# Splitting the first normalisation over two engines, and the last product into three token ranges

## The chip, the core and the metric

The kernel runs on one core of a Trainium2 chip. The core has a matrix engine (TensorE, PE in the rows; its weight loads are PEld), a vector engine (VectorE, DVE), a scalar engine (ScalarE, ACT), a general engine (GpSimd, POOL), and a sync engine (SyncE, SP) that issues transfers; ScalarE and GpSimd issue transfers too. Each engine runs its own instructions strictly in order and waits on semaphores for the others. The metric is the device time of one execution in microseconds, as the median of several runs.

## What is computed

One step of a two-layer decoder in float32, for a prompt of 1024 tokens and a sample group of 8 × 4 tokens with the same weights. The first layer mixes tokens by retention, the second by sliding-window attention; each sub-layer is normalised before and after, and each layer ends in a feed-forward block:

```python
def rms_norm(x, g):
    xf = x.astype(jnp.float32)
    y = xf * lax.rsqrt(jnp.mean(xf * xf, axis=-1, keepdims=True) + EPS)
    return y.astype(x.dtype) * g.astype(x.dtype)
...
def retention_layer(h, pos, state0, g_pre, w_in, w_out, g_post):
    x = rms_norm(h, g_pre)
    proj = x @ w_in
    ...
    return h + rms_norm(o @ w_out, g_post), S

def ffn(h, g_pre, w1, w2, g_post):
    u = jax.nn.relu(rms_norm(h, g_pre) @ w1)
    return h + rms_norm((u * u) @ w2, g_post)
```

D_MODEL is 1024, the hidden width 4096. The two places that matter here are the very first `rms_norm(h, g_pre)` of the retention layer, for the first half of the prompt, and the very last line, `h + rms_norm((u * u) @ w2, g_post)` of the second layer, for the second half of the prompt and the sample group.

## The kernel before

The prompt is cut into two halves of 512 tokens; the second half carries the 32 sample tokens along, so it has 544 columns. Activations lie with features on the partitions and tokens along the columns, in 8 tiles of 128 features. A float32 product is made of three products of a reduced format (`passes`): high part with high part, high with low, low with high. ScalarE casts a weight tile to its high part (`whi`, line 499), VectorE subtracts for the low part (`wlo`, line 500). `proj_fm` (line 527) issues the three passes for each of 4 or 8 weight tiles of an output tile. The order on each engine follows from program order, a scheduler that respects the waits, and generators (`side`, `tick`) that let side work advance between products. PSUM has four banks for accumulators (`mm`) and four for transposes and the like (`aux`).

**The start.** Eight products of zeros (`RATES["warm"]`, line 208) run first. `x_first` then normalises four chunks of 128 tokens: a square with a row sum on ScalarE (line 566), small steps on VectorE, the scaling of the chunk (line 572), then for each half `q` of the features four transposes on TensorE (line 554), the multiplication by the gain on VectorE (line 578, 128 × 512), the cast to the high part on ScalarE (line 580) and the low part on VectorE (line 581). The results of two chunks feed products of 256 columns. Next to it the first weights arrive and are split (lines 499, 500).

**The tokens.** Before the last product, `tokens_of_h` reads the residual of the second half back and transposes it (line 1052) to rows of tokens, chunk by chunk, eight transposes for each.

**The last product.** `finish` adds the last block of hidden features to the accumulated result `y`. It goes over two ranges of tokens, 0 to 272 and 272 to 544. For each range and each of 8 output tiles `m`: 12 products (line 527), the addition to `y` on VectorE (line 538), on ScalarE the result times the gain (line 1096) and its square (line 1098), on VectorE the sum of squares (line 1100). From the fourth tile on, `turn` transposes finished tiles (line 1065) into six banks, two for each of three chunks of tokens; those of tiles 5 to 7 come after the last product of a range. `close` then sums the squares over the partitions by products of one column (line 1070), computes the factor with one activation (line 1075) and three small steps (lines 1076 to 1078), and for each chunk makes two additions of 512 columns on VectorE (line 1081) and one store (line 1087), from SyncE or ScalarE in turn. The close of the first range is written after the second tile of the second range. The chunks are 96, 96 and 80 tokens in the first range, 120, 120 and 32 in the second.

Of the kernel before, what the change touches and what calls it, by code (L numbers as in the profile page):

```python
# [13 lines left out]
AF = mybir.ActivationFunctionType  # L14
# [5 lines left out]
P = 128  # L20
# [96 lines left out]
def body(ctx, tc,  # L117
# [11 lines left out]
    def f32(ap):  # L129
        return ap.bitcast(F32)  # L130
# [76 lines left out]
    for _ in range(RATES["warm"]):  # L207
        T.matmul(wps[:, :256], lhsT=zero[:, :P], rhs=zero, start=True, stop=True)
# [348 lines left out]
    def x_first(xs, rp):  # L557

        loads = [x_load(0, c) for c in range(2)]
        for c in range(4):  # L560
# [13 lines left out]
            for q in range(2):  # L574
                pv = x_transpose(xn, q, P)
                d = slice(c * P, (c + 1) * P)
                tmp = rp.tile([P, 512], F32, tag="ob", bufs=3, name="xg").rearrange("p (k t) -> p k t", k=4)
                V.tensor_tensor(out=tmp, in0=pv, in1=g_first[:, 4 * q:4 * q + 4].unsqueeze(2).to_broadcast([P, 4, P]),
                                op=ALU.mult)
                S.copy(out=xs[q][0][:, :, d], in_=tmp)  # L580
                V.tensor_tensor(out=xs[q][1][:, :, d], in0=tmp, in1=f32(xs[q][0][:, :, d]), op=ALU.subtract)
            yield
# [452 lines left out]
    def token_chunks(r):  # L1035
        c0, c1 = RANGES[1][r]
        cut = [c0, 96, 192, c1] if r == 0 else [c0, 392, HC, c1]
        return list(zip(cut, cut[1:]))

    def tokens_of_h():  # L1040
# [3 lines left out]
        for r, (c0, c1) in enumerate(RANGES[1]):  # L1044
            h = range_tile(c1 - c0)
            G.dma_start(out=h, in_=hD[1][:, :, c0:c1])
            for i, (t0, t1) in enumerate(token_chunks(r)):
                yield out
                for q in range(2):
# [3 lines left out]
                    (S.copy if q else V.tensor_copy)(out=out[3 * r + i][:t1 - t0, q], in_=ps[:t1 - t0])  # L1053
        yield out

    def finish(f, hT):
# [10 lines left out]
        def close(st):  # L1067
# [4 lines left out]
            for i, (t0, t1) in enumerate(st["chunks"]):  # L1072
# [10 lines left out]
                if t0 < HC:  # L1083
                    dst = y_prompt[0, HC + t0:HC + t1]
                else:
                    dst = y_sample.rearrange("b t d -> (b t) d")
                (nc.sync, nc.scalar)[i % 2].dma_start(out=dst.rearrange("t (a c) -> t a c", a=2), in_=ht[:n])

        prev = None
        for r, (c0, c1) in enumerate(RANGES[1]):  # L1090
            w = c1 - c0
            st = dict(c0=c0, chunks=token_chunks(r), yg=range_tile(w), i0=3 * r, acc=nt()[:, :w])
            for m in range(KT):
# [9 lines left out]
                if m == 3:  # L1103
                    banks = [auxps() for _ in range(4)] + [mmps() for _ in range(2)]
                    st["outs"] = [banks[2 * i:2 * i + 2] for i in range(3)]
                    turn(st, 0)
# [473 lines left out]
```

## Time and profile before

| What | us |
|---|---|
| Median of 3 runs | 2871.67 |
| Lowest and highest | 2870.13, 2872.47 |
| Profiled execution | 2868.01 |
| Its span | 2866.2 |
| TensorE busy | 2815.8 |
| VectorE busy | 1725.0 |
| ScalarE busy | 1319.3 |
| GpSimd busy | 180.6 |

The span lies inside the execution, from its first instruction to its end. TensorE is busy nearly throughout, so the page's totals say little about a change at the two ends. Those are read from the timeline, where each row is a run of like instructions with its start, its duration and, in brackets, how long the engine stood idle before it and what ended that. The mean granted clock of TensorE over the execution is 0.993 of full speed; the table by stretch tells where it was lower.

### The profile page before, as it was taken

To read this page: it belongs to the slowest core of one execution; us is meant where nothing else is said; L and a number is where in the kernel's file an instruction comes from. 1 tells how busy PE (TensorE), PEld (TensorE's weight loads), DVE (VectorE), ACT (ScalarE), POOL (GpSimd) and SP (SyncE) were. 2 spreads that over 40 slices of the span, in tenths; PEclk is the share of its full clock that TensorE was granted. 3 is DMA by queue.
4 is the path that set the end of the run, shared out by engine and by line. 5 is a ranking of instruction groups with operands and counts; after the bars stand their busy time and mean duration, and the time that the engine had idled before them with its cause. 6 is when DMAs were issued, how large, how long until landed. Compare 5 with 4: busy or idle time off the path is not lost.

```text
span 2866.2 us, 43419 instructions
## 1 busy us (share of the span) xinstructions
PE 2815.8 (98%) x17217; PEld 2474.9 (86%) x17217; DVE 1725.0 (60%) x3348; ACT 1319.3 (46%) x2556; POOL 180.6 (6%) x262
## 2 busy tenths in 40 slices
PE   8999999999999999999999999999999999999998
PEld 7888888888889799888998898888877788899998
DVE  5444566585575888773444664564547636987645
ACT  3343344343334556532544764345547734565422
POOL 2000000010010100000000000000010100001000
PEclk9999999999999999999999999999999999999999
DMA  6322242454353554653553432445533424555632
GB/s 208 95 84 85 84 133 85 147 168 160 126 190 114 198 161 143 193 184 98 165 166 128 135 93 74 126 134 178 170 116 111 126 80 128 151 156 173 211 115 68
DMA packets 418426, 391.14 MB, mean 136 GB/s; under 512 B 13879, under 2 KB 360287, under 8 KB 416175
## 3 DMA queue, kind: packets, MB, share of 16 engines
q1 hardware_dynamic: 380191, 248.97, 29.3%
q0 software_dynamic: 36848, 137.36, 13.5%
q8 instruction: 135, 2.21, 0.3%
q10 hardware_dynamic: 1183, 2.04, 0.2%
q14 instruction: 69, 0.56, 0.1%
HBM read 308.73 MB, written 79.56 MB: 135 GB/s over the span
## 4 chain that ended last, share of the span: by engine, by line
PE 87%; issue 5%; DVE 4%; ACT 2%; DMA 2%; POOL 0%; SPq 0%; DVEq 0%; ACTq 0%; POOLq 0%
PE mm L527 57%; PE mm L667 6%; PE mm L1151 4%; PE py L429 4%; PE px L429 3%; PE p L429 2%; PE aux L800 2%; PE aux L809 2%; PE aux L876 1%; PE aux L1309 1%; DVE wlo L500 1%; PE aux L885 1%; PE aux L718 1%; PE aux L744 1%; PE aux L1276 1%
## 5 line engine op out<-in xcount | busy, mean ns | idle before, releaser
L527 PE MATMUL mm<-x,whi 128*128 128x272 f32 (+2 forms) x7520 | 1652.3, 326 | 11.2 <-DVE y L538 6.2
L527 PEld LDWEIGHTS mm<-x,whi 128*128 128x128 f32 x7520 | 1189.1, 189 | 136.0 <-issue 10.2
L527 PE MATMUL mm<-x,wlo 128*128 128x272 f32 (+2 forms) x3760 | 1030.8, 325 | 0.6 <-DVE wlo L500 0.5
L500 DVE TENSOR_TENSOR wlo<-wraw,whi 128x1024 fp32r<-128x1024 f32 x346 | 422.8, 1223 | 474.6 <-ACT whi L499 474.0
L527 PEld LDWEIGHTS mm<-x,wlo 128*128 128x128 f32 x3760 | 635.2, 189 | 55.7 <-DVE wlo L500 1.5
L499 ACT CAST whi<-wraw 128x1024 fp32r<-128x1024 f32 x346 | 362.8, 1049 | 686.2 <-PE mm L527 549.8
L538 DVE TENSOR_TENSOR y<-y,mm 128x272 f32<-128x272 f32 (+1 forms) x264 | 131.2, 518 | 139.1 <-PE mm L527 138.3
L667 PE MATMUL mm<-whi,x 128*128 128x512 f32 x512 | 166.3, 396 | 0.0
L1151 PE MATMUL mm<-whi,x 128*128 128x512 f32 x384 | 124.2, 394 | 0.0
L667 PEld LDWEIGHTS mm<-whi,x 128*128 128x128 f32 x512 | 95.8, 188 | 22.8 <-DVE n L647 0.8
L667 PE MATMUL mm<-wlo,x 128*128 128x512 f32 x256 | 101.0, 394 | 0.0
L975 DVE TENSOR_TENSOR x<-x,x 128x1024 fp32r<-128x1024 f32 (+1 forms) x64 | 79.3, 1254 | 29.2 <-ACT x L974 29.1
L264 DVE TENSOR_TENSOR n<-n 128x272 f32<-128x272 f32 (+1 forms) x196 | 84.3, 430 | 9.1 <-ACT n L263 1.8
L1151 PEld LDWEIGHTS mm<-whi,x 128*128 128x128 f32 x384 | 72.1, 188 | 17.6
L429 PE MATMUL py<-x,y 128*128 128x272 f32 (+1 forms) x600 | 84.1, 289 | 0.2 <-DVE x L441 0.2
L429 PE MATMUL px<-x,whi 128*128 128x272 f32 (+1 forms) x400 | 75.5, 287 | 5.1 <-ACT whi L393 5.1
L429 PEld LDWEIGHTS py<-x,y 128*128 128x128 f32 x600 | 76.4, 188 | 3.0 <-DVE x L441 1.8
L1151 PE MATMUL mm<-wlo,x 128*128 128x512 f32 x192 | 75.7, 394 | 0.0
L974 ACT CAST x<-x 128x1024 fp32r<-128x1024 f32 (+1 forms) x64 | 67.0, 1076 | 17.9 <-DMA x<-uD 14.7
L505 DVE SCALAR_TENSOR_TENSOR wlo<-wraw,gall,whi 128x512 fp32r<-128x512 f32 x48 | 34.7, 748 | 59.8 <-ACT whi L504 59.6
L370 DVE TENSOR_TENSOR wlo<-x,whi 128x1024 fp32r<-128x1024 f32 x50 | 61.1, 1225 | 15.6 <-ACT whi L377 10.7
L373 DVE TENSOR_TENSOR x<-x 128x512 f32<-128x512 f32 x100 | 68.9, 689 | 1.6
(349 smaller groups left out, 3558.5 us busy)
## 6 DMA issues: line engine op xcount, KB each, us to landing
wraw<-in_ffn_w_dram SPq DMA_DIRECT2D x206, 512.0 KB, 3.9
wraw<-in_ret_w_in_dram SPq DMA_DIRECT2D x96, 512.0 KB, 3.8
x<-in_ffn_w_dram SPq DMA_DIRECT2D x50, 512.0 KB, 5.3
uD<-x POOLq DMA_DIRECT2D x32, 544.0 KB, 4.4
x<-uD POOLq DMA_DIRECT2D x16, 1088.0 KB, 6.4
wraw<-in_ret_w_out_dram SPq DMA_DIRECT2D x32, 512.0 KB, 3.5
x<-in_state_ret_dram SPq DMA_DIRECT2D x32, 512.0 KB, 5.7
out_dram<-x POOLq DMA_DIRECT2D x32, 512.0 KB, 3.5
```

Source lines behind the costliest of these rows:

```text
L264: V.tensor_tensor(out=acc, in0=acc, in1=sq, op=ALU.add)
L370: V.tensor_tensor(out=l, in0=r, in1=f32(h), op=ALU.subtract)
L373: V.tensor_tensor(out=r, in0=a, in1=b, op=ALU.add)
L429: T.matmul(ps, lhsT=w_, rhs=x_, start=k == 0 and i == 0, stop=k == 3 and i == 2)
L499: S.copy(out=hi, in_=raw)
L500: V.tensor_tensor(out=lo, in0=raw, in1=f32(hi), op=ALU.subtract)
L527: T.matmul(p_[:, :w], lhsT=a, rhs=b[:, o:o + w], start=(k == 0 and i == 0), stop=(k == n - 1 and i == 2))
L538: V.tensor_tensor(out=y[m][:, o:o + w], in0=y[m][:, o:o + w], in1=ps, op=ALU.add)
L667: T.matmul(ps[c][:a.shape[1]], lhsT=a, rhs=b, start=(k == 0 and i == 0), stop=(k == KT - 1 and i == len(prods) - 1))
L974: S.copy(out=hi[:, a:a + 2], in_=f32(lo)[:, a:a + 2])
L975: V.tensor_tensor(out=lo[:, a:a + 2], in0=f32(lo)[:, a:a + 2], in1=f32(hi)[:, a:a + 2], op=ALU.subtract)
L1151: T.matmul(ps[c][:a.shape[1]], lhsT=a, rhs=b, start=(k == 0 and i == 0), stop=(k == KT - 1 and i == len(prods) - 1))
```

## The change

At the start, a helper `idle(n)` issues products of zeros; four are issued after the transposes of each of the first three chunks of `x_first`, besides the eight at the very start. For the second half of the features (`q` = 1) the multiplication by the gain moves from VectorE to four ScalarE activations of 128 × 128 with a scale column; the first half stays on VectorE.

At the end, the two ranges become three (`ENDS`): tokens 0 to 208, 208 to 416 and 416 to 544, in two, two and one chunks of 104, 104, 104, 104 and 128. The result's banks are two for each chunk. The last chunk, which holds 96 prompt tokens and the 32 sample tokens, is stored in halves: after each addition of 512 columns, 96 rows from SyncE and 32 rows from ScalarE. `tokens_of_h` follows the same chunks, five instead of six, with three loads instead of two.

```diff
--- before.py
+++ after.py
@@ -204,8 +204,12 @@
     zero = nt(256)
     V.memset(zero, 0.0)
     wps = auxps()
-    for _ in range(RATES["warm"]):
-        T.matmul(wps[:, :256], lhsT=zero[:, :P], rhs=zero, start=True, stop=True)
+
+    def idle(n):
+        for _ in range(n):
+            T.matmul(wps[:, :256], lhsT=zero[:, :P], rhs=zero, start=True, stop=True)
+
+    idle(RATES["warm"])
     csm = cp.tile([P, c_small.shape[1]], F32, name="csm")
     nc.scalar.dma_start(out=csm, in_=c_small)
     ident = csm[:, 0:P]
@@ -575,10 +579,16 @@
                 pv = x_transpose(xn, q, P)
                 d = slice(c * P, (c + 1) * P)
                 tmp = rp.tile([P, 512], F32, tag="ob", bufs=3, name="xg").rearrange("p (k t) -> p k t", k=4)
-                V.tensor_tensor(out=tmp, in0=pv, in1=g_first[:, 4 * q:4 * q + 4].unsqueeze(2).to_broadcast([P, 4, P]),
-                                op=ALU.mult)
+                if q:
+                    for k in range(4):
+                        S.activation(out=tmp[:, k], in_=pv[:, k], func=AF.Copy, scale=g_first[:, 4 + k:5 + k])
+                else:
+                    V.tensor_tensor(out=tmp, in0=pv, in1=g_first[:, 0:4].unsqueeze(2).to_broadcast([P, 4, P]),
+                                    op=ALU.mult)
                 S.copy(out=xs[q][0][:, :, d], in_=tmp)
                 V.tensor_tensor(out=xs[q][1][:, :, d], in0=tmp, in1=f32(xs[q][0][:, :, d]), op=ALU.subtract)
+            if c < 3:
+                idle(4)
             yield
 
     def x_store(half, loads=None):
@@ -1032,25 +1042,23 @@
                 nc.sync.dma_start(out=dst, in_=ot[:n])
             yield
 
-    def token_chunks(r):
-        c0, c1 = RANGES[1][r]
-        cut = [c0, 96, 192, c1] if r == 0 else [c0, 392, HC, c1]
-        return list(zip(cut, cut[1:]))
+    ENDS = [[(0, 104), (104, 208)], [(208, 312), (312, 416)], [(416, 544)]]
 
     def tokens_of_h():
 
         ts = [x4(F32) for _ in range(3)]
         out = [ts[i // 2][:, 2 * (i % 2):2 * (i % 2) + 2, :512] for i in range(6)]
-        for r, (c0, c1) in enumerate(RANGES[1]):
+        for r, chunks in enumerate(ENDS):
+            c0, c1 = chunks[0][0], chunks[-1][1]
             h = range_tile(c1 - c0)
             G.dma_start(out=h, in_=hD[1][:, :, c0:c1])
-            for i, (t0, t1) in enumerate(token_chunks(r)):
+            for i, (t0, t1) in enumerate(chunks):
                 yield out
                 for q in range(2):
                     ps = auxps()
                     for k in range(4):
                         T.transpose(ps[:t1 - t0, k * P:(k + 1) * P], h[:, 4 * q + k, t0 - c0:t1 - c0], ident)
-                    (S.copy if q else V.tensor_copy)(out=out[3 * r + i][:t1 - t0, q], in_=ps[:t1 - t0])
+                    (S.copy if q else V.tensor_copy)(out=out[2 * r + i][:t1 - t0, q], in_=ps[:t1 - t0])
         yield out
 
     def finish(f, hT):
@@ -1080,16 +1088,19 @@
                 for q in range(2):
                     V.scalar_tensor_tensor(out=ht[:n, q], in0=st["outs"][i][q][:n], scalar=t, in1=ht[:n, q],
                                            op0=ALU.mult, op1=ALU.add)
-                if t0 < HC:
-                    dst = y_prompt[0, HC + t0:HC + t1]
-                else:
-                    dst = y_sample.rearrange("b t d -> (b t) d")
-                (nc.sync, nc.scalar)[i % 2].dma_start(out=dst.rearrange("t (a c) -> t a c", a=2), in_=ht[:n])
+                    if t1 > HC:
+                        cs = slice(q * 512, (q + 1) * 512)
+                        nc.sync.dma_start(out=y_prompt[0, HC + t0:2 * HC, cs], in_=ht[:HC - t0, q])
+                        nc.scalar.dma_start(out=y_sample.rearrange("b t d -> (b t) d")[:, cs], in_=ht[HC - t0:n, q])
+                if t1 <= HC:
+                    (nc.sync, nc.scalar)[i % 2].dma_start(
+                        out=y_prompt[0, HC + t0:HC + t1].rearrange("t (a c) -> t a c", a=2), in_=ht[:n])
 
         prev = None
-        for r, (c0, c1) in enumerate(RANGES[1]):
+        for r, chunks in enumerate(ENDS):
+            c0, c1 = chunks[0][0], chunks[-1][1]
             w = c1 - c0
-            st = dict(c0=c0, chunks=token_chunks(r), yg=range_tile(w), i0=3 * r, acc=nt()[:, :w])
+            st = dict(c0=c0, chunks=chunks, yg=range_tile(w), i0=2 * r, acc=nt()[:, :w])
             for m in range(KT):
                 acc_out(y, m, False, proj_fm(wb[m // 4], m % 4, us, [(c0, w)]))
                 ym = y[m][:, c0:c1]
@@ -1101,8 +1112,7 @@
                 if m == 1 and prev:
                     close(prev)
                 if m == 3:
-                    banks = [auxps() for _ in range(4)] + [mmps() for _ in range(2)]
-                    st["outs"] = [banks[2 * i:2 * i + 2] for i in range(3)]
+                    st["outs"] = [[auxps(), auxps()] for _ in chunks]
                     turn(st, 0)
                 if m > 3:
                     turn(st, m - 3)
```

Line numbers of the changed kernel are 4 higher near the start (line 527 becomes 531, 554 becomes 558) and 4 to 11 higher further on (538 becomes 542, 572 becomes 576, 578 becomes 586, 580 and 581 become 588 and 589, 1065 becomes 1073, 1081 becomes 1089, 1096, 1098 and 1100 become 1107, 1109 and 1111). The multiplication on ScalarE is line 584.

ScalarE at the start, from its first weight cast. `x_108` and `x_109` are the high parts of the two halves of the features, `xg` the normalised chunk times the gain. Before:

```order
L499 CAST whi<-wraw 128x1024
L580 CAST x_108<-xg 128x4x128
L499 CAST whi<-wraw 128x1024
L580 CAST x_109<-xg 128x4x128
L499 CAST whi<-wraw 128x1024
L580 CAST x_108<-xg 128x4x128
L580 CAST x_109<-xg 128x4x128
```

and now:

```order
L503 CAST whi<-wraw 128x1024
L584 ACTIVATE xg<-aux,g_first 128x128 x4
L588 CAST x_108<-xg 128x4x128
L503 CAST whi<-wraw 128x1024
L588 CAST x_109<-xg 128x4x128
L584 ACTIVATE xg<-aux,g_first 128x128
L588 CAST x_108<-xg 128x4x128
L584 ACTIVATE xg<-aux,g_first 128x128 x3
L588 CAST x_109<-xg 128x4x128
L503 CAST whi<-wraw 128x1024
```

The four multiplications of a chunk have come in ahead of its second cast, and both casts of the second chunk now stand before the third weight cast, where they stood behind it.

TensorE at the start; `n` is the tile of zeros, `x_112` and `x_114` the first two chunks of tokens. Before:

```order
L208 MATMUL aux<-n 128x256 x8
L554 MATMUL aux<-csm,x_112 128x128 x8
L554 MATMUL aux<-csm,x_114 128x128 x8
L527 MATMUL mm<-x_108,whi 128x256 x2
L527 MATMUL mm<-x_110,whi 128x256
L527 MATMUL mm<-x_108,wlo 128x256
```

and now:

```order
L210 MATMUL aux<-n 128x256 x11
L558 MATMUL aux<-csm,x_112 128x128 x8
L210 MATMUL aux<-n 128x256
L558 MATMUL aux<-csm,x_114 128x128 x8
L210 MATMUL aux<-n 128x256 x8
L531 MATMUL mm<-x_108,whi 128x256 x2
L531 MATMUL mm<-x_110,whi 128x256
```

Products of zeros stand between the transposes of the first two chunks and eight of them before the first real products.

VectorE in the last product, around the close of the first range: line 538 (now 542) adds a product to the result, lines 1081 (now 1089) are the additions of 512 columns of the close. Before:

```order
L538 TENSOR_TENSOR y<-y,mm 128x272 x2
L1076 TENSOR_TENSOR sm<-sm 96x1
L1077 SCALAR_TENSOR_TENSOR sm<-mm,sm 96x1
L1078 SCALAR_TENSOR_TENSOR sm<-sm 96x1
L1081 SCALAR_TENSOR_TENSOR x_25494<-aux,sm,x_25494 96x512
L1100 TENSOR_TENSOR n<-n 128x272
L1081 SCALAR_TENSOR_TENSOR x_25494<-aux,sm,x_25494 96x512
L1076 TENSOR_TENSOR sm<-sm 96x1
L538 TENSOR_TENSOR y<-y,mm 128x272
L1077 SCALAR_TENSOR_TENSOR sm<-mm,sm 96x1
L1078 SCALAR_TENSOR_TENSOR sm<-sm 96x1
L1081 SCALAR_TENSOR_TENSOR x_25494<-aux,sm,x_25494 96x512 x2
```

and now:

```order
L542 TENSOR_TENSOR y<-y,mm 128x208 x2
L1084 TENSOR_TENSOR sm<-sm 104x1
L1085 SCALAR_TENSOR_TENSOR sm<-mm,sm 104x1
L1086 SCALAR_TENSOR_TENSOR sm<-sm 104x1
L1089 SCALAR_TENSOR_TENSOR x_25518<-aux,sm,x_25518 104x512
L1111 TENSOR_TENSOR n<-n 128x208
L1089 SCALAR_TENSOR_TENSOR x_25518<-aux,sm,x_25518 104x512
L1084 TENSOR_TENSOR sm<-sm 104x1
L1085 SCALAR_TENSOR_TENSOR sm<-mm,sm 104x1
L1086 SCALAR_TENSOR_TENSOR sm<-sm 104x1
L1089 SCALAR_TENSOR_TENSOR x_25518<-aux,sm,x_25518 104x512 x2
L542 TENSOR_TENSOR y<-y,mm 128x208
```

Before, the addition for the third tile of the second range stands between the first chunk's and the second chunk's additions; now it stands behind all four of the close.

## Rows read from the trace of the kernel before

**Rows 1.** The page: busy time, share of the span and instruction count of each engine.

```profile
PE 2815.8 (98%) x17217; PEld 2474.9 (86%) x17217; DVE 1725.0 (60%) x3348; ACT 1319.3 (46%) x2556; POOL 180.6 (6%) x262
```

**Rows 2.** Timeline of the first 25 us: start, us, engine, line, operation, out<-in, count [idle before].

```profile
8.70 1.09 PE L554 MATMUL aux<-csm,x 128*128 128x128 f32 x8 [2.08 <-DVE x L572]
...
10.55 1.04 ACT L499 CAST whi<-wraw 128x1024 fp32r<-128x1024 f32 x1 [1.02 <-DMA wraw<-in_ret_w_in_dram]
...
14.18 1.97 PE L554 MATMUL aux<-csm,x 128*128 128x128 f32 x8 [4.38 <-DVE x L572]
...
15.78 1.28 DVE L578 TENSOR_TENSOR xg<-aux,g_first 128x512 f32<-128x512 f32 x2
...
16.66 1.04 ACT L499 CAST whi<-wraw 128x1024 fp32r<-128x1024 f32 x1 [2.92 <-DMA wraw<-in_ret_w_in_dram]
17.61 1.13 ACT L580 CAST x<-xg 128x512 fp32r<-128x512 f32 x2
...
19.62 0.58 PE L527 MATMUL mm<-x,whi 128*128 128x256 f32 x1 [0.54 <-DVE x L581]
...
24.91 2.03 PE L554 MATMUL aux<-csm,x 128*128 128x128 f32 x16
```

**Rows 3.** Eight stretches: length, busy time of five engines, granted PE clock, DMA share, GB/s.

```profile
12.00:18.00 6.00, 1.97 (x8) 1.57 (x8) 5.32 (x8) 3.02 (x5) 0.00 (x0) 0.50 0.63 198
18.00:25.00 7.00, 6.18 (x27) 5.89 (x28) 4.50 (x13) 3.34 (x8) 0.00 (x0) 0.50 1.02 358
25.00:30.00 5.00, 5.00 (x45) 5.00 (x44) 4.34 (x8) 1.83 (x4) 0.00 (x0) 0.99 0.03 11
53.00:56.00 3.00, 1.53 (x7) 0.94 (x5) 1.38 (x2) 0.00 (x0) 1.41 (x2) 1.00 0.92 242
2262.00:2264.00 2.00, 0.00 (x0) 0.00 (x0) 1.86 (x12) 1.82 (x10) 0.00 (x0) 1.00 0.46 105
2264.00:2268.00 4.00, 2.95 (x9) 2.28 (x10) 3.60 (x14) 2.35 (x6) 0.78 (x1) 0.54 0.74 215
2332.50:2336.00 3.50, 3.50 (x23) 2.91 (x22) 0.00 (x0) 0.41 (x2) 0.00 (x0) 0.99 0.57 150
2336.00:2339.00 3.00, 3.00 (x14) 2.95 (x14) 1.16 (x5) 1.62 (x8) 0.00 (x0) 0.50 0.02 6
```

**Rows 4.** Groups by form on ScalarE: busy us, mean ns; a multiply by a scale column.

```profile
L1423 ACT ACTIVATE sel<-sel,sm 128x128 f32<-128x128 f32 x128 | 40.8, 393 | 4.3 <-DVE sm L1421 4.1
```

**Rows 5.** Timeline of TensorE: two bursts of 128-column products, two products of 512 columns.

```profile
1624.35 1.11 PE L1272 MATMUL aux<-y,x 128*128 128x128 f32 x8
1625.30 0.71 PE L527 MATMUL mm<-x,whi 128*128 128x272 f32 x4
...
1632.58 1.00 PE L1272 MATMUL aux<-y,x 128*128 128x128 f32 x8
1633.42 0.71 PE L527 MATMUL mm<-x,whi 128*128 128x272 f32 x4
...
2330.68 0.39 PE L527 MATMUL mm<-x,wlo 128*128 128x512 f32 x1
2330.91 0.62 PE L527 MATMUL mm<-x,whi 128*128 128x512 f32 x2
```

**Rows 6.** Timeline of the last 20 us: products, accumulates and closes.

```profile
2846.43 4.79 PE L527 MATMUL mm<-x,x 128*128 128x272 f32 x36
...
2851.30 1.75 PE L527 MATMUL mm<-x,x 128*128 128x272 f32 x12
2851.46 0.43 DVE L538 TENSOR_TENSOR y<-y,mm 128x272 f32<-128x272 f32 x1
...
2853.17 0.43 DVE L538 TENSOR_TENSOR y<-y,mm 128x272 f32<-128x272 f32 x1
...
2856.78 1.41 DVE L1081 SCALAR_TENSOR_TENSOR x<-aux,sm,x 120x512 f32<-120x512 f32 x2
...
2860.54 1.39 DVE L1081 SCALAR_TENSOR_TENSOR x<-mm,sm,x 32x512 f32<-32x512 f32 x2
```

## The prediction

> **What bounds the kernel now.** I read the page's busy times first [rows 1]: TensorE is busy 98% of the span. Time can therefore be won or lost only where TensorE runs, waits, or runs at its lower clock, and at the two ends, where something else carries the chain. The order of instructions moves only there: in the first 50 us, in the token transposes before the last product, and in that product with its stores. So I read the timeline of the first 25 us [rows 2], then the table by stretch for TensorE's granted clock [rows 3], then the durations of forms that the change introduces [rows 4, 5], and last the timeline of the final 25 us [rows 6]. At the start the reader should see TensorE stand idle before the second set of transposes and again before the first real products, and then run 7 us at a granted clock of 0.50, the lower of its two levels (1.2 of 2.4 GHz). At the end the reader should see TensorE finish about 13 us before the span does, while VectorE closes three chunks in turn.
>
> The profiled execution took 2868.0 us with a span of 2866.2 us; the median of the runs is 2871.7 us. I sum against the profiled execution and carry the difference over to the median.
>
> **The start.** Before, ScalarE's third weight cast waits for its weights until 16.66, the casts of the second token chunk queue behind it at 17.61, and VectorE's low part follows; the third product starts at 19.62 [rows 2]. In the new order the second chunk's normalisation on VectorE comes before the gain multiply of the first, and both casts of the second chunk come before that third weight cast. The chain on ScalarE is then: first weight cast until 11.6; four multiplies of 0.32 (a form with the same shape and a scale column takes 40.8/128 = 0.32 each [rows 4]); cast 0.6; weight cast 1.04; cast 0.6; one multiply 0.32; cast 0.6 [rows 2]. That ends at 16.0, and VectorE's low part of about 0.7 and the semaphores put the third product at about 17.2. Gain: 2.4 us. What VectorE sheds is four multiplies of 0.64 [rows 2], none of which TensorE waits for in full.
>
> The products of zeros cost nothing where TensorE would wait anyway. Before, it does 1.09 and 1.97 us of transposes between 8 and 18 us and nothing else [rows 2], and the granted clock reads 0.50 over 12 to 18 and on until 25 [rows 3]. Twelve added products, about 5 us at the lower clock, fill that hole. If the clock is up when the real products come, the 24 products from 19.62 to 24.91, 0.22 each [rows 2], run at the pace of the stretch 25 to 30, 45 products and transposes in 5.00 us [rows 3], 0.12 at most: 24 × (0.22 − 0.12) = 2.4 us. Against that, transposes now wait for VectorE at the third and fourth chunk, and ScalarE's extra eight multiplies for those chunks (2.6 us) stand before casts that are waited for: together some 1.8 us, an estimate. Sum of the start: −2.4 − 2.4 + 1.8 = **−3.0 us**. If the clock does not come up even by 25, the second term goes, and some 26 products of the stretch 25 to 30 cost 0.11 more each: −2.4 + 1.8 + 2.9 = **+2.3**. The later loads of this stretch go into tiles that TensorE's own transposes release, so they move along with it, and I count nothing for them.
>
> **The token transposes.** Five chunks instead of six, eight transposes each: 8 × 0.11 = **−0.9 us**. One more load of 104 or 128 columns on the GpSimd queue starts long before its reader.
>
> **The last product: the array's own time.** It is 24 products for each of 8 output tiles: 12 on each of two ranges of 272 columns before, 36 on ranges of 208, 208 and 128 after. So 192 instructions become 288. At 272 columns one costs (4.79 − 1.75)/24 = 0.127 us [rows 6], or 24.4 us for all. What one of 128 columns costs is in the same kernel: eight products of 128 columns take from 1624.35 to 1625.30, 0.119 each, and a second such burst, at 1632.58, 0.105 [rows 5]. I take 0.112. That is hardly less than the 0.11 to 0.12 of 256 columns [rows 3]: halving the columns does not halve the time, so something that every instruction pays sets it. For 208 columns the cost lies between 0.11 and 0.12; I take 0.112 too. After: 192 × 0.112 + 96 × 0.112 = 32.3 us, so **+7.9 us** (+5.8 at 0.105, +9.9 at 0.119). The Trainium skill, page "TensorE: Matmul & The Clock Gate", section "LDWEIGHTS (loading the stationary operand)", puts a weight load at columns/1.2 ns, 107 ns for the 128 columns of every load here, whatever streams past it; by that the 288 instructions would take 30.8 us. The bursts of [rows 5] agree with it within a tenth.
>
> Transposes of the result: 40 instead of 48, −0.9.
>
> **The last product: the accumulate chain and the closes.** Each tile passes VectorE's add, two ScalarE activations and VectorE's second add before VectorE takes the next: 1.71 us from 2851.46 to 2853.17, for 272 columns [rows 6]. VectorE's forms of 512 columns take 0.64 and of 272 columns 0.43 [rows 2, 6], about 0.001 us a column; with the same for ScalarE the four operations shrink by 0.004 a column, so 1.46 us at 208 and 1.16 at 128; TensorE needs 12 × 0.112 plus two transposes, 1.56, and 1.45. The chain hardly regains anything once it is late. And it is made late: the new VectorE order runs all four 512-column multiply-adds of the previous range (0.70 each [rows 6]) with their small steps, two chunks of 1.9 us and a narrow addition, 4.2 us, before the accumulate of the third tile, and ScalarE's store issue, which waits for the same multiply-adds, stands before that tile's activation. Before, that accumulate went in after one of the chunks. TensorE runs four accumulators ahead and then waits. At the end of the second range it has the transposes of tiles 5, 6 and 7 in front of the third range's products, each waiting for its tile's activation: about 3.3 us of waits, with only six transposes and a few products in some 4 us. Together with the waits at the end I count **+3.1 us** over before.
>
> **The tail.** Before, from VectorE's last accumulate at 2853.17 the statistics come through at 2856.78, then three chunks of 1.9 us each, to 2861.93; the last store and the end take 4.27 more: 13.0 in all [rows 6]. After, one chunk is left: 3.6 less 0.7 for narrower operations and fewer one-column products, then two multiply-adds, 1.4, then the same 4.3, since the store after the first half lands earlier than that of the second: 8.6. **−4.4 us.**
>
> With the clock up the last product is 7.9 − 0.9 + 3.1 − 4.4 = +5.7.
>
> **The clock in the third range.** This decides it. The granted clock stays at 1.00 through 2262 to 2264 with TensorE idle and reads 0.54 in the next 4 us, and products there run slowly although TensorE has work again. It fell also at 2336, after 3.5 us in which TensorE was busy throughout, with 23 instructions, most of them narrow [rows 3]. It did not fall at 53 to 56, with 1.53 of 3 us busy [rows 3]. The wait before the third range is nearer to the first of these; what follows is 128-column products, nearer to the second. I take the clock to fall, and not to come back: at 0.50 it stayed from 18 to 25 under a stream of 256-column products that was almost without gaps [rows 3]. At the lower clock eight transposes of 128 columns take 1.97 us against 1.09 [rows 2], so the 96 products and 8 transposes of the third range, 11.6 us, take 11.6 more, less the 2.3 us of waits at its end that slower products hide: **+9.3 us**. The Trainium skill, same page, section "HAM oscillation — how this bites in real kernels", says that a wait between bursts sends the array back to its half-rate clock, so that the next burst starts slow. [rows 3] shows that at 2262 and not at 53.
>
> **Sum.** −3.0 − 0.9 + 5.7 + 9.3 = +11.1; 2871.7 + 11 = **2882.5 us**, rounded.
>
> **The rivals.** *The clock holds.* If the tile activations come sooner than I think, or the gap is split as at 53 to 56, the third range runs at full speed: −3.0 − 0.9 + 5.7 = +1.8, 2873.5 us, no change. For it: the wait is made of three shorter ones with transposes between. Against it: narrow products alone brought it down at 2336. [...]
>
> *The products' time follows their columns.* A product of 512 columns follows the one before by 0.23 [rows 5], one of 272 by 0.127; the slope gives 0.10 for 208 and 0.065 for 128: 25.4 us, +1.0 instead of +7.9, with one more us of waits as the chain then binds: 2867.6 with the clock up. That is not slower than before. It decides at the price of a 128-column product: below 0.09 it holds. The same page, section "Back-to-back issue gap", has a bare gap of columns/2.4 + 2.5 ns, 89 and 56 ns, that is 22.5 us, by which the change would win outright; the page itself calls this too low where weights are loaded each time, and [rows 5] speaks against it.
>
> *The start does not get its clock.* Then the start is +2.3 and the sum 2887.8. For it: at 18 to 25 the clock stayed low for 7 us of products.
>
> **How the numbers follow.** Forecast 0.55, clock holds 0.25, columns 0.08, start without its clock 0.08 (on top of the forecast), and 0.04 for something else. The forecast's own size is uncertain by the product price (±2) and by how much of the third range is slow (−4 to +1). The range runs from 2869, under the rival with the clock up, to 2886.5; the column rival and most of the slow start are left out. 0.2% of 2872 is 5.7 us, about what a measurement of this kernel can tell from no change. Faster by more: the column rival's better half and unforeseen gains, 0.08. Within: the clock rival and half of the column rival, 0.29. Slower by more: 0.63.
>
> **What would show it.** In the changed kernel: the third product at about 17 us and a granted clock near 1.0 from 18 to 25; products of 208 and 128 columns spaced 0.11 at full clock; a wait of TensorE for the activations of the last three tiles before the third range; a granted clock of 0.50 in the last 20 us and products there at 0.22; one pair of 512-column multiply-adds after the last product. I am wrong if the 128-column products come at 0.06, if the clock in the third range reads 1.0, or if TensorE's first real products still come after 19 us.

## The result, and the profile after

| | before | changed |
|---|---|---|
| Median at first, us | 2871.05 (4 runs) | 2889.79 (4 runs, 2886.63 to 2892.15) |
| Ratio, 95% interval | | 1.006 (1.0048 to 1.0072) |
| Measured again | 2872.28 (9 runs) | 2888.79 (5 runs), ratio 1.0059 (1.0046 to 1.0073) |
| Span of the profiled execution | 2866.2 | 2889.5 |

The change costs 17 to 19 us where 11 were forecast, and the time lies above the range. The direction and the mechanism were right; a term that was counted as a gain of 3 us is no gain in the whole kernel.

The page of the changed kernel, the line that answers to [rows 1]. TensorE has 102 instructions more and 28 us more of busy time: it works as constantly as before, has more to do and does it more slowly.

```profile
PE 2843.9 (98%) x17319; PEld 2500.6 (87%) x17319; DVE 1722.9 (60%) x3353; ACT 1326.0 (46%) x2586; POOL 182.2 (6%) x263
```

The start, TensorE's timeline of the changed kernel (answers to [rows 2]):

```profile
8.87 1.09 PE L558 MATMUL aux<-csm,x 128*128 128x128 f32 x8 [1.04 <-DVE x L576]
...
11.74 1.26 PE L558 MATMUL aux<-csm,x 128*128 128x128 f32 x8 [1.34 <-DVE x L576]
12.83 3.62 PE L210 MATMUL aux<-n 128*128 128x256 f32 x16
16.10 0.59 PE L531 MATMUL mm<-x,whi 128*128 128x256 f32 x2
17.01 0.39 PE L531 MATMUL mm<-x,whi 128*128 128x256 f32 x1 [0.32 <-DVE x L589]
```

and the table by stretch (length, busy time and count of PE, PEld, DVE, ACT and POOL, TensorE's granted clock, DMA share, GB/s; answers to the first three of [rows 3]):

```profile
12.00:18.00 6.00, 5.68 (x34) 4.88 (x33) 5.64 (x8) 5.62 (x14) 0.00 (x0) 1.00 0.61 190
18.00:25.00 7.00, 6.49 (x54) 6.08 (x54) 5.47 (x15) 4.63 (x12) 0.00 (x0) 1.00 1.01 352
25.00:30.00 5.00, 4.78 (x38) 4.16 (x37) 4.82 (x12) 3.18 (x8) 1.56 (x2) 1.00 0.16 64
```

The third product starts at 17.01 instead of 19.62, the products of zeros (two records in the trace for each) fill the wait, and the clock reads 1.00 where it read 0.50. At 60 us the same products come 2.9 us earlier than before.

The last product, TensorE's timeline (answers to [rows 6]; the brackets are waits for the activation of the tile that is to be transposed):

```profile
2836.75 1.57 PE L531 MATMUL mm<-x,x 128*128 128x208 f32 x12
2838.16 0.38 PE L1073 MATMUL aux<-csm,x 128*104 128x128 f32 x2
...
2856.70 0.43 PE L1073 MATMUL aux<-csm,x 128*104 128x128 f32 x2 [0.85 <-ACT x L1107]
2858.16 0.67 PE L1073 MATMUL aux<-csm,x 128*104 128x128 f32 x2 [1.03 <-ACT x L1107]
2858.48 0.67 PE L531 MATMUL mm<-x,x 128*128 128x128 f32 x2
2859.61 0.67 PE L1073 MATMUL aux<-csm,x 128*104 128x128 f32 x2 [0.47 <-ACT x L1107]
2859.94 4.94 PE L531 MATMUL mm<-x,x 128*128 128x128 f32 x22
...
2870.57 2.80 PE L531 MATMUL mm<-x,x 128*128 128x128 f32 x12
2873.17 0.43 PE L1073 MATMUL aux<-csm,x 128*128 128x128 f32 x1
```

Twelve products of 208 columns take 1.41 us, from 2836.75 to the next transpose, 0.1175 a product. Ahead of the third range three waits of 0.85, 1.03 and 0.47 us stand with two products between. Then twelve products of 128 columns take 2.60 us (2870.57 to 2873.17), 0.217 each. The table by stretch says why:

```profile
2850.00:2855.00 5.00, 4.31 (x39) 4.13 (x38) 1.81 (x6) 1.75 (x5) 0.00 (x0) 1.00 0.60 170
2855.00:2860.00 5.00, 2.65 (x17) 1.97 (x16) 2.11 (x7) 2.66 (x8) 0.00 (x0) 0.80 0.00 0
2860.00:2865.00 5.00, 5.00 (x27) 5.00 (x25) 0.61 (x3) 0.60 (x2) 0.00 (x0) 0.50 0.00 0
2870.00:2875.00 5.00, 5.00 (x26) 5.00 (x26) 1.46 (x6) 1.20 (x4) 0.00 (x0) 0.50 0.54 155
```

In the stretch with the waits the mean clock is 0.80, and from there it is 0.50 to the end, though TensorE is busy for 5.00 of every 5 us. VectorE shows what made the waits, and the short tail:

```profile
2848.82 1.41 DVE L1089 SCALAR_TENSOR_TENSOR x<-aux,sm,x 104x512 f32<-104x512 f32 x2
2850.14 0.36 DVE L542 TENSOR_TENSOR y<-y,mm 128x208 f32<-128x208 f32 x1
...
2881.47 0.29 DVE L542 TENSOR_TENSOR y<-y,mm 128x128 f32<-128x128 f32 x1 [1.44 <-PE mm L531]
...
2884.33 1.41 DVE L1089 SCALAR_TENSOR_TENSOR x<-aux,sm,x 128x512 f32<-128x512 f32 x2
```

All four additions of the first range's close run before the addition of the second range's third tile, which comes at 2850.14. After the last accumulate, at 2881.47, only one pair of additions is left. From the last product's first instruction to the end of the span the changed kernel takes 59.7 us, before 44.0.

What was not expected lies between. The same instructions in the same order ran at the lower clock in other places than before. Four stretches of the changed kernel:

```profile
1622.00:1627.00 5.00, 5.00 (x31) 5.00 (x30) 3.83 (x8) 3.46 (x5) 0.00 (x0) 0.66 0.00 0
1714.00:1719.00 5.00, 4.41 (x23) 3.27 (x24) 2.53 (x6) 2.82 (x9) 0.00 (x0) 0.66 0.00 1
1888.00:1893.00 5.00, 2.91 (x24) 2.69 (x23) 5.00 (x15) 3.82 (x13) 0.00 (x0) 1.00 0.43 155
2329.00:2334.00 5.00, 5.00 (x22) 4.33 (x21) 1.49 (x7) 1.66 (x5) 0.00 (x0) 0.66 0.02 3
```

and the same times in the kernel before:

```profile
1622.00:1627.00 5.00, 4.22 (x30) 3.26 (x30) 2.90 (x7) 4.85 (x14) 0.00 (x0) 1.00 0.01 3
1714.00:1719.00 5.00, 4.66 (x37) 3.91 (x37) 2.88 (x8) 3.89 (x12) 0.00 (x0) 1.00 0.36 109
1888.00:1893.00 5.00, 5.00 (x30) 5.00 (x30) 3.53 (x9) 1.92 (x4) 0.00 (x0) 0.66 0.27 72
2329.00:2334.00 5.00, 5.00 (x29) 4.05 (x28) 2.85 (x7) 2.16 (x7) 0.00 (x0) 1.00 0.21 48
```

### The profile page after: what moved, and what is told of

Read it like the earlier page. It is cut to its first block, busy times and chain, and to the rows that moved or that the text cites. A ratio compares the mean times of both kernels' runs of the same rounds, so it can differ in the third digit from the quotient of the medians.

```text
span 2889.5 us, 43671 instructions
## 1 busy us (share of the span) xinstructions
PE 2843.9 (98%) x17319; PEld 2500.6 (87%) x17319; DVE 1722.9 (60%) x3353; ACT 1326.0 (46%) x2586; POOL 182.2 (6%) x263
## 4 chain that ended last, share of the span: by engine, by line
PE 86%; issue 5%; DVE 5%; ACT 2%; DMA 2%; POOL 0%; ACTq 0%; SPq 0%; DVEq 0%; POOLq 0%
PE mm L531 56%; PE mm L677 6%; PE mm L1161 4%; PE py L433 4%; PE px L433 3%; PE p L433 2%; PE aux L810 2%; PE aux L819 2%; DMA wraw<-in_ffn_w_dram 1%; PE aux L886 1%; DVE wlo L504 1%; PE aux L1319 1%; PE aux L895 1%; PE aux L728 1%; PE aux L1286 1%
## 5 line engine op out<-in xcount | busy, mean ns | idle before, releaser
L542 DVE TENSOR_TENSOR y<-y,mm 128x272 f32<-128x272 f32 (+3 forms) x272 | 132.0, 506 | 147.0 <-PE mm L531 146.1
L509 DVE SCALAR_TENSOR_TENSOR wlo<-wraw,gall,whi 128x512 fp32r<-128x512 f32 x48 | 34.7, 748 | 59.8 <-ACT whi L508 59.6
```

The source lines that it names most:

```text
L542: V.tensor_tensor(out=y[m][:, o:o + w], in0=y[m][:, o:o + w], in1=ps, op=ALU.add)
```

## The experiments

Two theories at first. *Theory 1*: the last product costs what its trace shows, some 15 us; the rest of the loss, which lies between 1600 and 2800 us, comes from the lead of the start, which moves thin stretches to places where the clock falls. *Rival*: the end part also causes the loss in the middle.

**The two halves of the change, and pure delays.** `start_only` is the change up to and with `x_first`; `end_only` is the rest of the diff. `shift2`, `shift6` and `start_shift12` add 2, 6 and 12 useless products ahead of the same point, shown with 2:

```diff
+                            if half == 0 and h == 1 and c == k == i == 0:
+                                for _ in range(2):
+                                    T.matmul(ps[c], lhsT=a, rhs=b, start=True, stop=True)
                             T.matmul(ps[c][:a.shape[1]], lhsT=a, rhs=b, start=(k == 0 and i == 0),
```

> Only the start is changed; the tokens and the last product are those of before. In the changed kernel TensorE led by 2.9 us at 60 us and had lost 11.7 us against before by 2640 us, with no instruction moved in between. Theory 1 (displacement): the lead itself moves the thin stretches in the middle, the granted clock falls at other and more places, so this kernel loses the same 11.7 us: -2.9 + 11.7 = +8.8, about 2880 us, ratio 1.003. Rival (the end part causes the loss in the middle, for instance by its tiles or its loads): -2.9, about 2868 us, ratio 0.999.

> Only the tokens and the last product are changed; the start is that of before. Theory 1 (displacement): the middle is before's, the last product loses 15.7 us as in the changed kernel and the token transposes give back 1.2: +14.5, about 2885.5 us, ratio 1.005, with the clock low throughout the third range. Rival (the end part causes the loss in the middle): +14.5 + 11.7 = +26, about 2897 us, ratio 1.009.

> The changed start alone, and in the second head's value product, near 100 us, the first product of 512 columns is issued twelve times more into a bank that the real one then overwrites: 12 x 0.231 = 2.8 us of useless work, which takes the start's lead away again. Theory 1 (displacement): the middle stands where it stood in before, the clock falls where it fell there, and the total is before's: -2.9 + 2.8 + 0 = -0.1, about 2871 us, ratio 1.000, faster than the start alone by some 9 us although it does more. Rival (the changed start costs in the middle by itself, wherever that stands): +8.8 + 2.8 = +11.6, about 2883 us, ratio 1.004.

> The kernel before with two useless products of 512 columns in the second head's value product: 0.46 us of work, nothing else changed. Theory 1 (displacement): whether the clock falls in a thin stretch depends on where the stretch stands, so even this can add or take falls; anything from +0.5 to +12 us, with a list of falls in the profile that differs from before's. Rival (the loss is tied to the changed start or end): +0.5 us, 2871.5 us, ratio 1.000, and the same falls as before.

> Before with six useless products of 512 columns in the second head's value product, 1.39 us, nothing else changed. Theory 1 in its narrower form (what the thin stretches of the middle cost depends on where they stand, and a changed start puts them in a worse place): the net of the delay is not zero, as the changed start lost some 4 us in the middle; a total 3 to 6 us above before, 2874 to 2877 us. Rival (the middle differs from one execution to the next and does not depend on where it stands): 1.4 us above before, 2872.5 us.

| Kernel | us, median | Before, same chip | Ratio, 95% interval |
|---|---|---|---|
| start_only | 2872.93 (11 runs) | 2870.82 (27) | 1.0008 (0.9999 to 1.0016) |
| end_only | 2885.95 (5) | 2870.82 | 1.0053 (1.0040 to 1.0065) |
| start_shift12 | 2872.95 (11) | 2870.82 | 1.0010 (1.0001 to 1.0019) |
| shift2 | 2871.95 (11) | 2870.82 | 1.0005 (0.9996 to 1.0014) |
| shift6 | 2872.99 (11) | 2871.64 (21) | 1.0006 (0.9997 to 1.0014) |

The end part alone costs 15.1 us, as forecast for it, and in its profile the middle is not slower than elsewhere: the rival falls. `start_only` lies between the 2880 us of Theory 1 and the 2868 of the rival. The 27 runs of before showed what three had not: one and the same kernel takes 2867 to 2877 us. The table by stretch of each profile shows the clock fall in the middle at four to eight places, not the same ones each time. The profile of before was a lucky one: against it the same product near 2740 us comes 2 to 8 us late in every other kernel, after every known difference is taken off 1 to 11 us. So the 11.7 us that single profiles put on the middle are for the most part a difference between executions. For Theory 1 in the form of a place that decides nothing speaks either: `shift6` costs the 1.4 us of its own work where 3 to 6 were expected, though its interval reaches to 4, and `start_shift12`, which takes the lead away again, comes out like `start_only` and not at before's time. What stands is that the changed start does not make the whole kernel faster.

**Which part of the start.** `zeros_only` leaves the gain multiply on VectorE, `share_only` leaves out `idle(4)`.

> Before with the twelve added products of zeros, the gain multiply left on VectorE for both halves. Theory: the granted clock is 1.0 when the real products start, and the 24 products that ran at 0.22 us run at 0.12: -2.4 us at 60 us, third product still at 19.6. If the total follows that, 2868.5 us; the start alone has shown that a lead of this size can be gone by the end, and if the thin stretches in the middle take it back again the total lies at 2870 to 2873. Rival (the zeros delay the products behind them): 0 to +2 us at 60 us.

> Before with the gain multiply of the second half of the features on ScalarE, without added products of zeros. Theory: the third product comes at 17.2 instead of 19.6, but the granted clock is 0.50 as before and stays there until some wide products have run, and the later chunks wait for ScalarE: between -1 and +2.3 us at 60 us, total 2870 to 2874 us. Rival (the sharing gains its 2.4 us whatever the clock): -2.4 us at 60 us.

`zeros_only` took 2872.71 us against 2871.28, ratio 1.0005 (0.9996 to 1.0014); `share_only` 2872.22, ratio 1.0002 (0.9993 to 1.0011). By stretch, and in one row of TensorE's timeline, the zeros alone:

```profile
12.00:18.00 6.00, 5.31 (x32) 4.69 (x31) 5.18 (x8) 3.26 (x6) 0.00 (x0) 1.00 0.65 228
18.00:25.00 7.00, 5.86 (x47) 5.38 (x47) 5.43 (x16) 4.62 (x9) 0.00 (x0) 1.00 0.79 253
```
```profile
16.77 0.38 PE L531 MATMUL mm<-x,whi 128*128 128x256 f32 x1 [0.69 <-DVE x L585]
```

and the sharing alone:

```profile
12.00:18.00 6.00, 2.30 (x9) 1.91 (x10) 4.69 (x7) 4.43 (x12) 0.00 (x0) 0.64 0.69 206
18.00:25.00 7.00, 7.00 (x37) 6.78 (x36) 3.49 (x11) 3.57 (x8) 0.00 (x0) 0.57 0.99 352
```

The zeros alone hold the clock at 1.00 and bring the third product to 16.77: without a change in the gain multiply the new order, with the second chunk's normalisation drawn forward, is there too. The sharing alone leaves the mean clock at 0.64 and 0.57 in these stretches, brings the third product to 18.4 instead of the expected 17.2, and gains nothing by 60 us. What the start gains is the zeros' doing, and neither shows in the total. The zeros do not hold the clock in every execution: in the profile of `start_only` it reads 0.72 over 12 to 18, the third product comes at 19.1, and at 100 us only 0.7 us of lead are there.

**Where the start's gain goes.** Four pairs of the kernel before and the changed start, three of them cut off with a `return`: behind the retention layer, behind the first half's attention, behind the second half's.

> Before, cut off after the retention layer: the feed-forward blocks, the attention layer and all outputs behind them are left out, about 1050 to 1100 us are left. In no profile so far did the granted clock fall between 100 and 1600 us, so this kernel holds the start and a stretch in which nothing drifts. It is the base for the next one; no theory differs on it.

> The changed start, cut off at the same place (the feed-forward blocks, the attention layer and the outputs behind them are left out). Theory 1 (the start gains, the thin stretches of the middle take it back): 2 to 3 us less than the cut-off kernel before, while the whole kernel with the changed start took 2 us more. Rival (the lead seen in single profiles is not there on the mean): within 0.7 us of the cut-off kernel before.

> Before, cut off after the first half's attention and the block beside it, near 1890 us; what follows, and the outputs of it, are left out. Base for the next one.

> The changed start, cut off at the same place near 1890 us (the rest is left out). At 1030 us the changed start led by 2.5 us. Theory (the loss comes with the first thin stretches, those of the first half's attention between 1610 and 1890 us): the lead is down to 0 or turned into +1. Rival (it comes later): still -2.5.

> Before, cut off after the second half's attention and the block beside it, near 2480 us; what follows, and the outputs of it, are left out. Base for the next one.

> The changed start, cut off at the same place near 2480 us (the rest is left out). Theory (each group of thin stretches takes a part): between 0 and +2 us. Rival (the loss is behind this place, in the wait at 2490 us or the end): -2.5. Second rival (there is no loss, the whole kernels differed by chance): -2.5 here as well as at the first cut.

| Cut at | Before's start, us | Changed start, us | Difference |
|---|---|---|---|
| 1030 | 1028.99 (1028.39 to 1029.45, 5 runs) | 1026.44 (1025.82 to 1026.59, 4) | −2.5 |
| 1900 | 1906.14 (1902.19 to 1908.15, 4) | 1904.73 (1903.82 to 1905.95, 4) | −1.4 |
| 2470 | 2472.17 (2469.89 to 2473.34, 4) | 2472.76 (2470.36 to 2474.22, 5) | +0.6 |
| whole | 2870.82 (27) | 2872.93 (11) | +2.1 |

At 1030 us the gain is there in every run and the two do not overlap. Behind the first attention the runs spread over 6 us and overlap, and at 2470 us the lead is gone. So it is real, and it is lost between 1600 and 2500 us, where TensorE waits and the clock falls now here, now there. Why this stretch costs more with the changed start than without is open for the larger part. It is not more time at the lower clock: twice the shortfall of the mean granted clock from 1, times the span, gives 46 us at the lower level for before and 35 for `start_only`, which is the 10 us that the start itself saves. And neither a delay of 0.5 nor one of 1.4 us costs the like, as far as intervals of about 2.6 us either way tell. With two to ten us of spread the two last differences of the table are each within chance. That the lead does not arrive is not: a whole kernel that is 2.5 us faster has a ratio of 0.9991, and the intervals of `start_only` and `zeros_only` begin at 0.9999 and 0.9996.

One part of the loss can be read from the profiles. Near 1843 us ScalarE waits for a load of weights, and TensorE behind it. Before:

```profile
1843.64 1.05 ACT L499 CAST whi<-wraw 128x1024 fp32r<-128x1024 f32 x1 [2.17 <-DMA wraw<-in_ffn_w_dram]
1856.41 0.49 PE L527 MATMUL mm<-x,whi 128*128 128x272 f32 x2 [3.23 <-DVE y L538]
```

and `start_only`, with the one transfer of instructions (queue q8: packets, MB, share) that runs between 1840.2 and 1846:

```profile
1846.06 1.05 ACT L503 CAST whi<-wraw 128x1024 fp32r<-128x1024 f32 x1 [3.96 <-DMA wraw<-in_ffn_w_dram]
1858.82 0.79 PE L531 MATMUL mm<-x,whi 128*128 128x272 f32 x2 [5.02 <-DVE y L542]
q8 instruction: 1, 0.02, 1.3%
```

In the nine profiles without the added products of zeros that reach this place, ScalarE waits 2.2 us here and TensorE 3.2 to 3.3; in seven of the eight with them it is 3.4 to 4.0 and 4.4 to 5.0. Between 1840 and 1862 us these seven fall 2.6 to 4.0 us back against the profile of before, the others at most 1.5. So a load does not move along with its readers here: the two that are issued just before, at the same place in the program, land 7.1 and 7.3 us later in `start_only` and 5.3 and 5.6 in before, where the transfer of instructions comes only after them. That these collide is argued, not tested; in the eighth profile the transfer runs there too, and ScalarE's wait stays at 2.2. On the mean it is some 2 of the 4.6 us between the first and the last row of the table.

**The clock ahead of the third range.**

```diff
+            if r == 1:
+                hold = mmps()
+                ha, hb = wb[0](0, 0)[0], us[0][0]
             for m in range(5, KT):
                 turn(st, m)
+                if r == 1:
+                    for _ in range(7):
+                        T.matmul(hold[:, :256], lhsT=ha, rhs=hb[:, :256], start=True, stop=True)
```

> The changed last product and tokens with before's start, and during the wait ahead of the third range seven useless products of 256 columns behind each of the transposes of tiles 5, 6 and 7, into a bank that nobody reads. Theory 1 (TensorE's thin stretch ahead of the third range drops the clock): the granted clock reads 1.0 through the third range, its products come 0.11 us apart instead of 0.215, and the last product takes some 9 us less than with the changed end alone: about 2876.5 us against 2886, ratio to before 1.002. Rival (128-column products drop the clock or are slow by themselves): the clock is at 0.50 in the third range all the same, 2886 to 2888 us, ratio 1.005 to 1.006.

Measured: 2879.9 us, ratio to before 1.0030 (1.0018 to 1.0041), 6.0 us less than `end_only`. TensorE's timeline, and the table by stretch:

```profile
2852.85 0.43 PE L1063 MATMUL aux<-csm,x 128*104 128x128 f32 x2 [0.85 <-ACT x L1097]
2853.03 1.07 PE L1116 MATMUL mm<-x,x 128*128 128x256 f32 x7
...
2856.86 2.79 PE L527 MATMUL mm<-x,x 128*128 128x128 f32 x24
2859.49 0.47 PE L1068 MATMUL mm<-csm,n 128*104 128x1 f32 x4
```

```profile
2855.00:2860.00 5.00, 4.80 (x44) 4.60 (x43) 1.16 (x4) 1.34 (x4) 0.00 (x0) 1.00 0.00 0
2860.00:2865.00 5.00, 5.00 (x47) 5.00 (x47) 4.38 (x14) 1.61 (x6) 0.00 (x0) 1.00 0.15 33
```

With 21 useless products in the wait the clock stays at 1.00 to the end of the products and 24 products of 128 columns take 2.63 us from 2856.86, 0.110 each, half of what they took. That settles both disputed points: it is the thin stretch that drops the clock, and narrow products neither drop it here nor run faster than 0.11. The last product takes 52.0 us of the span against 58.9 in `end_only`; of the 9.4 us that the products of the third range gain, a wait at the end and the useless products take 2.5 back.

**Without narrow products.** `two_ranges` keeps five chunks and the split store and goes back to two ranges; this is the line that decides, the rest of its diff puts tiles into other buffers and splits loads in two:

```diff
-    ENDS = [[(0, 104), (104, 208)], [(208, 312), (312, 416)], [(416, 544)]]
+    ENDS = [[(0, 96), (96, 192), (192, 288)], [(288, 416), (416, 544)]]
```

> Before's start; the last product in two ranges of 288 and 256 tokens, with three chunks of 96 and two of 128, the last one stored in halves; a range's intermediate tiles lie in two buffers instead of one. It keeps the changed kernel's five chunks and its split store, and leaves out the narrow products. Theory (the price of an instruction, not the columns, makes the three ranges dear): 96 x (0.134 + 0.119) = 24.3 us of products, as before, no thin stretch, one chunk of 1.9 us less at the end, 16 transposes less: -3.5 us, about 2867.5 us, ratio 0.999. Rival (the third range's short tail is what an early end needs, or the closes delay the second range as in the changed kernel): no better than before, 2871 or more.

> The two ranges of 288 and 256 tokens, five chunks and split store, with the changed start. Theory 1: the start's gain is lost in the middle as in the whole kernel with the changed start, about +2 us against the two ranges alone: 2870.5 us, ratio to before 1.000. Rival (the start gains 2 us and the loss in the middle was chance): 2866 us, ratio 0.998, the fastest version so far.

`two_ranges` took 2868.31 us, ratio 0.9987 (0.9978 to 0.9996): 0.1% less than before, just clear of its interval, and less than the changed kernel. With the changed start it took 2869.13, ratio 0.9992 (0.9983 to 1.0000), no better. VectorE at its end:

```profile
2856.22 0.41 DVE L538 TENSOR_TENSOR y<-y,mm 128x256 f32<-128x256 f32 x1
...
2859.66 1.41 DVE L1081 SCALAR_TENSOR_TENSOR x<-aux,sm,x 128x512 f32<-128x512 f32 x2
...
2861.55 1.41 DVE L1081 SCALAR_TENSOR_TENSOR x<-aux,sm,x 128x512 f32<-128x512 f32 x2
```

From the last accumulate, 2856.22, two pairs of additions remain where before had three [rows 6]; the last product takes 41.8 us against 44.0.

**The changed kernel again.**

> The changed kernel once more, beside before on one chip. The parts measured so far add up to +2 (start) and +15 (end): 2888 us, ratio 1.006. If the granted clock falls in the third range in this execution as well, the last product takes 59 to 60 us from its first product to the end of the span, against 43.5 to 43.9 in every kernel with before's end. Rival (the fall in the third range was chance): about 2880 us, and a last product of 50 to 52 us.

2888.79 us. In this execution, too, the clock fell ahead of the third range and stayed down, and the last product took 59.8 us.

## Why the prediction was wrong, and where it was right

**Right: the last product.** Forecast +15.0 us in all; 58.9 to 59.8 us against 44.0 is +15 to +16. A product of 128 columns costs 0.110 at full clock, one of 208 0.1175 (0.112 was taken for both). The waits stand where the order put them, 2.4 us for the 3.3 of the forecast. The tail is 8.0 us from the last accumulate against 13.0, −5 for −4.4. The clock fell ahead of the third range and stayed low. The Trainium skill, page "TensorE: Matmul & The Clock Gate", section "HAM oscillation — how this bites in real kernels", says that a wait between bursts makes the next burst start at the half-rate clock. `end_hold` agrees: with the wait filled the products cost 0.110 us, behind the bare waits, none longer than 1.03 us, 0.217.

**Right in size, at its place, in part by luck: the start.** −3.0 forecast; −2.9 at 60 us in this profile, −2.5 on the mean at the first cut. But the 2.4 us of the earlier third product were put down to the sharing, which alone brings it only to 18.4 and gains nothing by 60 us; the zeros alone bring it to 16.77. The tokens gave back 0.9 for 0.9.

**Wrong: that a lead at 60 us is a lead at the end.** The step is the sum, which adds the start's −3.0 to the end's terms and puts the 2700 us between at nothing. The one reason that the prediction gives for a lead to last, that later loads move along "and I count nothing for them", is given for the loads of the start, and there it held: up to 1600 us the lead is whole. It does not hold further on, where near 1843 us a load lands up to 1.8 us late with TensorE waiting for it, and where the clock falls now here, now there; the runs with the changed start took 1 to 2 us more instead of 2.5 less. Beyond that load the cause stays open. That is 4 to 5 of the 6 to 7 us by which the forecast fell short. The rest is the last product, one us dearer, and chance: before and changed kernel each spread over some 8 us, so that two sets of runs gave +18.7 and +16.5.

**The rivals.** "The clock holds" did not come, though [rows 3] had a case for it; `end_hold` shows that it would have been worth 6 us and not 9. That case, 53 to 56, was chance: it is one wait of 2.86 us, not a split one, TensorE waits 2.1 to 3.0 us there in all nineteen profiles, and in eleven of them the clock falls to 0.50 there. "Time follows the columns" fell. "The start does not get its clock" fell as it was written, but its result, a start that gives nothing, came about in another way, and there lay the mistake in the range: 0.08 for a start that does not pay, because the range was built from the cases of each term and not from how far one kernel's own runs lie apart. The three runs then at hand lay within 2.3 us, 28 later ones within 10.

## What to carry to other kernels

Before a product is cut into narrower ranges, find in the trace what an instruction costs that hardly streams: here 0.11 to 0.12 us for anything from 128 to 256 columns, so a third range costs half as many instructions again and its short tail cannot pay for that. Ask of each new boundary between bursts how long the array waits there, since at the lower clock the products behind it cost double (0.217 us for 0.110); some useless products in the wait are a cheap trial. And a gain of a tenth of a per cent at the start of a long kernel is not the kernel's: cut the kernel off behind the change to see whether the gain is real, and run the whole to see whether it arrives. A load further on that does not move along with the engines can take it back.

## What the runs showed of the hardware that was not expected

- One kernel's runs lie 10 us apart (2866.2 to 2876.4 in 28), and the granted clock falls in different stretches in each profile. Cut off at 1030 us, behind the falls of the start and ahead of the others, the same kernel's runs lie within 1.1 us.
- The clock stayed at 0.50 for over 20 us in which TensorE was busy without a gap, with products of 128 columns at 0.217 us each. In the kernel before it was back at 0.99 from 25 us on, with products of 256 columns [rows 3].
- 21 useless products of 256 columns in the wait, some 2.6 us of work, saved 6 us.
- What a fall of the clock costs depends on where it comes. In the profile of the changed start cut off at 1900 us the clock reads 0.50 around 1614 and TensorE is 2.1 us ahead of before at 1610 and again at 1640; it reads 0.50 around 1717, and the 2.1 us of lead at 1710 are 1.3 us of delay at 1725.
